# Differential attention's query and key projections ahead of the outputs of gated linear attention, its values and the gate and modulation columns among those outputs

## The chip, the cores and the metric

The kernel runs on one core of one Trainium2 chip. The metric is the time of one execution in device microseconds. The engines are named as in the profile: PE is the matrix engine (PEld its weight loads), DVE the vector engine, ACT the scalar engine, POOL the GpSimd engine, and SP the engine that here only issues transfers.

## What is computed

Two transformer blocks, one after the other, on 512 tokens of width 1024. The part that the change touches is the mixer of the first block. One projection of the normalised tokens (and of 256 context tokens) gives the inputs of two mixers: gated linear attention (GLA, 4 heads), which is evaluated in chunks with a state that decays, and differential attention (4 heads), which is a difference of two softmaxes over 256 + 512 keys.

```python
parts = project(h, w_in)   # gq, gk, gv, gr, gdown, dq, dk, dv
_, _, og = gla_bidir(qg, kg, vg, gf, gb, s_f, s_b)         # forward and backward scan
qd, kd, vd = diff_qkv(parts, q_norm_g, k_norm_g)           # RMS norm of queries and keys
qd, kd = apply_axial_rope(qd, cos, sin), apply_axial_rope(kd, cos, sin)
od = diff_attend(qd, concat(kd_c, kd), concat(vd_c, vd), lam)
mix = concat(gla_merge(og, r), diff_merge(od)) @ w_out     # r is a gate: silu
x = x + gt1 * mix                                          # gt1: a modulation column
```

Modulation columns are the rows of `silu(c) @ w_mod + b_mod`; shifts and scales of the first norm are made at the start, the other 32 columns of 128 in eight jobs of four.

## The kernel before

Matrix products are done in three terms (high and low halves of both sides, rounded to a reduced format): a weight tile is loaded by SP into a ring of two buffers (`wf`), cast by ACT to the high half (`whi`, line 186), and subtracted by DVE to the low half (`wlo`, line 187); those two have rings of three.

The stretch in question has three stages on the time axis.

- The **GLA gates and states** (lines 724 to 814). Gates of the context and of four chunks of 128 tokens, decays, and the states between chunks, in steps that each wait for ACT, DVE and POOL.
- The **GLA outputs** (lines 821 to 920). Sixteen units, one for each chunk and head. A unit takes decays by matrix products (`out_exp`, first line 829), exponentials on ACT (838), products on POOL and DVE (852, 855, 856), a score matrix in 32-column pieces (868 to 878), its assembly (882 to 890), and the output product (898, 899). The products of unit u + 1 are issued before the output of unit u.
- The **differential attention** (lines 924 to 1160 or so). For each head the queries and keys are stacked and transposed (`head_qk`), then 16 steps (4 heads x 4 blocks of 128 queries) of scores, exponentials and outputs; the last instruction of a step's output is the copy of line 1025.

All three leave PE room, and that room is filled from one list, `fillers`, of pairs (cost in us, job). `fill_in(us)` adds its allowance to what is left over and takes jobs off the front while the sum is at least half the cost of the next one. The list in order:

- 32 projection jobs of 24 matrix products of 256 columns each (`tm_job`, lines 284 to 286): keys (`w_dk`, 2 halves x 6 token tiles), values (`w_dv`), queries (`w_dq`, 2 halves x 4 tiles). A key or query job ends in a square on ACT (597), a sum (598), a scaling (602) and, for the tokens that are rotated, one product on DVE (609) and two on POOL (608, 611). A value job ends in one copy on ACT.
- four jobs for the GLA gate `r` (`w_gr`), 24 products of 512 columns each, with three ACT passes and a DVE product (671) at the end.
- modulation jobs (`mod_job`, 331 to 340), eight products in 32 columns of the array and four transposes, with four transfers of 512 KB through the same ring `wf`. `GM` gives the places in the list at which they are inserted; the rest come among the memory inputs (`MM`) and at the end of the list of the attention stage.

`fill_in(8)` stands once behind the context states, `fill_in(FC)` behind each of the four chunk steps, and `FG` is the allowance of an output unit. What is left behind the last unit, less one job, is issued at once; then the attention stage goes on with allowance `FA` a step and its own list (memory keys and values, merges, parts of the output projection).

Of the kernel before, what the change touches and what calls it, by code (L numbers as in the profile page):

```python
# [19 lines left out]
KT = D // 128  # L20
# [7 lines left out]
NLEV = 7  # L28
RW = 1088
GH = 0  # L30
FA, FG, FC, A0, GM, AM, AP = 3.4, 4.6, 3.0, 2, (16, 26), 0, ()
NF = 2
T0 = 1
T1 = 3
NP = 3
FS = 0.6
MM = (0, 1, 3, 5, 7)
NR = 1
GV = 0
PL = 3  # L40
# [21 lines left out]
HO = 0  # L62
# [18 lines left out]
def kernel(ctx: ExitStack, tc: tile.TileContext, a: dict, out: bass.AP, stop=None):  # L81
# [90 lines left out]
    def wsplit(src, n, lo_eng=None, dst=None, shape=None):  # L172
        wf = None if dst is None else dst[2]
        if wf is None:
            wf = ring.tile([128, RW], F32, tag="wf", name="wf", bufs=2)
        if shape is None:
            nc.sync.dma_start(wf[:, :n], src)
        else:
            nc.sync.dma_start(wf[:, :n].rearrange("p (m k c) -> p m k c", m=shape[0], k=shape[1]), src)
        if dst is None:  # L180
            hi = ring.tile([128, RW], F32R, tag="whi", name="whi")
            lo = ring.tile([128, RW], F32R, tag="wlo", name="wlo")
        else:
            hi, lo = dst[:2]
        tc.cur_priority -= WO
        A.copy(hi[:, :n], wf[:, :n])  # L186
        (lo_eng or V).tensor_tensor(lo[:, :n], wf[:, :n], f32(hi[:, :n]), ALU.subtract)  # L187
        tc.cur_priority += WO
        return hi, lo
# [3 lines left out]
    def mm3(o, lhi, llo, rhi, rlo, start, stop):  # L193
        tc.cur_priority += pe_late[0]
        T.matmul(o, lhi, rhi, start=start, stop=False)  # L195
        T.matmul(o, lhi, rlo, start=False, stop=False)  # L196
        ins = T.matmul(o, llo, rhi, start=False, stop=stop).ins  # L197
        tc.cur_priority -= pe_late[0]
        return ins
# [6 lines left out]
    def step():  # L206

        while between:
            try:
                return next(between[0])  # L210
            except StopIteration:
                between.pop(0)

    def drain():
        while between:
            step()

    def fm(w, ms, nk, bhi, blo, alloc, evac, segs=FULL, lo_eng=None, after=None, keep=None, every=4,
           have=None):


        def chunk(m, k0):
            if nk == 4:
                hi, lo = wsplit(w[m // 2].rearrange("p m k c -> p (m k c)"), 1024, lo_eng, keep and keep())
                have[m + 1, 0] = hi[:, 512:], lo[:, 512:]
                return hi, lo
            kn = min(8, nk - k0)
            return wsplit(w[m, :, k0:k0 + kn, :].rearrange("p k m -> p (k m)"), kn * 128, lo_eng, keep and keep())

        have = {} if have is None else have  # L230
        for a_, b_ in segs:
            for m in ms:
                p = alloc(m)
                for k in range(nk):
                    c = (m, k // 8)
                    if c not in have:
                        have[c] = chunk(m, k // 8 * 8)
                    hi, lo = have[c]
                    sl = slice(k % 8 * 128, k % 8 * 128 + 128)
                    mm3(p[:, a_:b_], hi[:, sl], lo[:, sl], bhi(k)[:, a_:b_], blo(k)[:, a_:b_], k == 0, k == nk - 1)  # L240
                    if k % every == every - 1 and k < nk - 1:
                        step()
                evac(m, a_, b_, p[:, a_:b_])
                step()
            if len(segs) > 1:
                drain()
                if after is not None:
                    between.append(after(a_, b_))
# [21 lines left out]
    def tm_load(w, half, n, lo_eng=None):  # L270

        ch = [wsplit(w[half, kc].rearrange("p k n -> p (k n)"), 4 * n, lo_eng) for kc in range(2)]

        def get(k):
            hi, lo = ch[k // 4]
            sl = slice((k % 4) * n, (k % 4 + 1) * n)
            return hi[:, sl], lo[:, sl]
        return get
# [83 lines left out]
    with tc.tile_pool(name="st", bufs=1) as st, tc.tile_pool(name="st2", bufs=2) as st2:  # L362
# [40 lines left out]
        def gq_weights(kc):  # L403

            return wsplit((a["w_gq"][:, :, 4 * kc:4 * kc + 4, :]).rearrange("m p k c -> p m k c"), 1024, shape=(2, 4))

        def gk_weights(kc):
            dst = None
            if kc:
                dst = [wk.tile([128, 1024], F32R, name=f"wk{i}") for i in range(2)] + [None]  # L410
            return wsplit(a["w_gk"][0, kc].rearrange("p k n -> p (k n)"), 1024, dst=dst)
# [51 lines left out]
        w = w0  # L463
        part = projected(0, w0)
        ins = mod_tiles(10)
        for k0 in (2, 4, 6):
            ins = queued(ins, lambda: next(part))
            ins = queued(ins, lambda: mod_tiles(k0))
            if k0 == 4:
                w = gq_weights(1), gk_weights(1)  # L470
# [146 lines left out]
    fillers = []  # L617
    got = {}

    def tm_job(w, hf, t, take, first):  # L620
        def run():
            if first:
                got[w, hf] = tm_load(a[w], hf, 256)
            p = acc()
            if t < 2:
                tm_tile(p[:, :256], got[w, hf], tok(chi, t), tok(clo, t))
            else:
                tm_tile(p[:, :256], got[w, hf], tok(hx, t - 2), tok(hxl, t - 2))
            take(hf, t, p[:, :256], slice(hf * 256, (hf + 1) * 256))
        return run  # L630
# [24 lines left out]
            V.tensor_scalar(rq[:, :, 4 * hf:4 * hf + 4], qk_rms("q", 4).rearrange("p (t h) -> p t h", t=4), 0.125, None, ALU.mult)  # L655

    jobs = [("w_dk", hf, range(6), take_k) for hf in range(2)]
    jobs += [("w_dv", 0, range(2), take_v), ("w_dv", 1, range(6), take_v), ("w_dv", 0, range(2, 6), take_v)]
    jobs += [("w_dq", hf, range(2, 6), take_q) for hf in range(2)]
    for w, hf, ts_, take in jobs:  # L660
        for t in ts_:
            fillers.append((2.6, tm_job(w, hf, t, take, t == ts_[0])))

    got_rs = []

# [4 lines left out]
        sigmoid(e, p)  # L670
        V.tensor_tensor(got_rs[0][:, m], p, e, ALU.mult)
    for m in range(4):
        fillers.append((5.2, lambda m=m: fm(a["w_gr"], [m], KT, hx, hxl, accs, silu_r)))

    def mod_job(n):
        def load(k):
            t = ring.tile([128, RW], F32, tag="wf", name="wm", bufs=2)[:, :1024]
            nc.sync.dma_start(t, a["w_mod"][n, k // 4, :, k % 4:k % 4 + 2].rearrange("p k n -> p (k n)"))
            return t
        return lambda: mod_block(16 + 4 * n, 4, load, mid2)  # L680
    mod_jobs = [(2.6, mod_job(n)) for n in range(8)]
    for at in GM:
        fillers.insert(at, mod_jobs.pop(0))
    left = [0.0]
    late_by = [HO]

    def fill_in(us):

        left[0] += us
        while fillers and left[0] >= 0.5 * fillers[0][0]:  # L690
            cost, run = fillers.pop(0)
            pe_late[0] = late_by[0]
            run()
            pe_late[0] = 0
            left[0] -= cost

    gla_scope = ExitStack()
    gp = gla_scope.enter_context(tc.tile_pool(name="gp", bufs=1))
    gt = gla_scope.enter_context(tc.tile_pool(name="gt", bufs=2))
# [55 lines left out]
    for h in range(4):  # L755
        hs = slice(h * 128, (h + 1) * 128)
        for jt in range(2):
            T.matmul(pU[:, hs], KTs[jt][:, hs], gvc[:, jt, hs], start=jt == 0, stop=jt == 1)
    fill_in(8)

    pg = s2()
    for h in range(4):
# [364 lines left out]
    for k in range(KT):  # L1127
        fillers.append((0.0, lambda k=k: mem_in(k)))
        if k in MM:
            fillers.append(mod_jobs.pop(0))  # L1130
# [699 lines left out]
```

## Time and profile before

| | us |
|---|---|
| median of 3 runs | 1685.4 (1685.23 to 1686.72) |
| the profiled execution | 1684.5 |
| its span, first to last instruction | 1682.7 |
| PE busy in the span | 1608.6 |
| DVE busy | 954.0 |
| ACT busy | 721.7 |
| POOL busy | 385.8 |

Durations below come from the one profiled execution, whose own time is 1684.5 us. PE's busy time counts pipelined products that overlap, so a busy PE can still have room; the distance between the starts of two products is the better measure of what one costs.

### The profile page before, as it was taken

Reading aid. Unit: us, or ns where it says so; the run is one execution under the profiler, and the core shown is the slowest. Engines: PE = TensorE matmul, PEld = TensorE weight load, DVE = VectorE, ACT = ScalarE, POOL = GpSimd, SP = SyncE. Lnnn points to the kernel's source line nnn. Section 1 sums busy time; section 2 is a strip of 40 time slices with the busy share of each in tenths; the row PEclk is TensorE's granted clock in tenths of the full one; section 3 lists DMA queues with packets and bytes.
Section 4 is the critical chain, followed back from the end, with each engine's and each line's share of the span. In section 5 each row is a group of like instructions: output and inputs, shape, how many; then the busy total and the mean of one; then the engine's idle time right before and its main releaser. Section 6 shows DMA issues by size and latency. Waiting matters only on the chain. (4 is left out here: it accounts for less than half of the span.)

```text
span 1682.7 us, 25345 instructions
## 1 busy us (share of the span) xinstructions
PE 1608.6 (96%) x9988; PEld 1355.8 (81%) x9988; DVE 954.0 (57%) x1678; ACT 721.7 (43%) x1372; POOL 385.8 (23%) x402
## 2 busy tenths in 40 slices
PE   8999898989999999999999999999888899999997
PEld 6898787658789888888889777888888888888886
DVE  6548878677656122222335675445677877776233
ACT  4444454567635322232233665234456544444221
POOL 1325546331112221210004000132423222221002
PEclk9999999999999999999999999999899899999998
DMA  9210212353523233323332212335110232333332
GB/s 376 67 48 26 87 55 88 95 188 117 164 78 114 75 101 100 100 91 91 98 111 73 77 37 72 89 99 177 49 36 29 76 99 91 99 99 95 95 91 73
DMA packets 47176, 160.88 MB, mean 96 GB/s; under 512 B 5456, under 2 KB 10064, under 8 KB 45264
## 3 DMA queue, kind: packets, MB, share of 16 engines
q1 hardware_dynamic: 44464, 156.69, 29.8%
q10 hardware_dynamic: 2304, 2.29, 0.4%
q8 instruction: 79, 1.29, 0.3%
q0 software_dynamic: 288, 0.28, 0.1%
q14 instruction: 41, 0.34, 0.1%
HBM read 156.36 MB, written 3.15 MB: 95 GB/s over the span
## 5 line engine op out<-in xcount | busy, mean ns | idle before, releaser
L186 ACT CAST whi<-wf 128x1024 fp32r<-128x1024 f32 (+3 forms) x219 | 226.6, 1036 | 429.2 <-PE acc L196 287.8
L187 DVE TENSOR_TENSOR wlo<-wf,whi 128x1024 fp32r<-128x1024 f32 (+3 forms) x181 | 225.8, 1248 | 180.0 <-ACT whi L186 174.6
L195 PE MATMUL acc<-qhi,whi 128*128 128x512 f32 (+1 forms) x640 | 240.9, 376 | 0.0
L196 PE MATMUL acc<-qlo,whi 128*128 128x512 f32 (+1 forms) x640 | 240.4, 376 | 0.0
L197 PE MATMUL acc<-qhi,wlo 128*128 128x512 f32 (+1 forms) x640 | 240.2, 375 | 0.0
L187 POOL TENSOR_TENSOR wlo<-wf,whi 128x1024 fp32r<-128x1024 f32 x38 | 91.1, 2397 | 209.7 <-ACT whi L186 209.7
L196 PEld LDWEIGHTS acc<-qlo,whi 128*128 128x128 f32 x640 | 122.3, 191 | 19.8 <-issue 0.2
L195 PEld LDWEIGHTS acc<-qhi,whi 128*128 128x128 f32 x640 | 122.3, 191 | 19.7
L197 PEld LDWEIGHTS acc<-qhi,wlo 128*128 128x128 f32 x640 | 122.2, 191 | 19.4
L196 PE MATMUL s<-qlo,whi 128*128 128x512 f32 (+1 forms) x336 | 127.5, 380 | 0.0
L195 PE MATMUL s<-qhi,whi 128*128 128x512 f32 (+1 forms) x336 | 127.5, 379 | 0.0
L197 PE MATMUL s<-qhi,wlo 128*128 128x512 f32 (+1 forms) x336 | 127.3, 379 | 0.0
L1293 DVE TENSOR_TENSOR e<-e,s 128x512 f32<-128x512 f32 (+1 forms) x22 | 14.3, 652 | 153.7 <-PE s L197 153.5
L196 PE MATMUL acc<-glo,whi 128*128 128x512 f32 (+1 forms) x208 | 74.3, 357 | 0.1
L195 PE MATMUL acc<-ghi,whi 128*128 128x512 f32 (+1 forms) x208 | 74.4, 358 | 0.0
L197 PE MATMUL acc<-ghi,wlo 128*128 128x512 f32 (+1 forms) x208 | 74.2, 357 | 0.0
L197 PEld LDWEIGHTS s<-qhi,wlo 128*128 128x128 f32 x336 | 63.2, 188 | 11.8
L195 PEld LDWEIGHTS s<-qhi,whi 128*128 128x128 f32 x336 | 63.2, 188 | 11.8
L196 PEld LDWEIGHTS s<-qlo,whi 128*128 128x128 f32 x336 | 63.2, 188 | 11.8
L195 PE MATMUL acc<-Fhi,whi 128*128 128x512 f32 (+1 forms) x187 | 71.5, 383 | 0.0
L196 PE MATMUL acc<-Flo,whi 128*128 128x512 f32 (+1 forms) x187 | 71.5, 383 | 0.0
L197 PE MATMUL acc<-Fhi,wlo 128*128 128x512 f32 (+1 forms) x187 | 71.5, 382 | 0.0
(643 smaller groups left out, 3994.9 us busy)
## 6 DMA issues: line engine op xcount, KB each, us to landing
wf<-in_w_ffn_in SPq DMA_DIRECT2D x44, 512.0 KB, 3.6
wf<-in_w_up SPq DMA_DIRECT2D x44, 512.0 KB, 3.5
wm<-in_w_mod SPq DMA_DIRECT2D x32, 512.0 KB, 4.1
wm<-in_w_mod SPq DMA_DIRECT2D x8, 1024.0 KB, 13.6
wf<-in_w_ffn_out SPq DMA_DIRECT2D x16, 512.0 KB, 3.5
wf<-in_w_g SPq DMA_DIRECT2D x16, 512.0 KB, 3.6
wf<-in_w_down SPq DMA_DIRECT2D x16, 512.0 KB, 3.5
X<-in_xT SPq DMA_DIRECT2D x4, 1024.0 KB, 5.0
```

What stands on the lines that cost most here:

```text
L186: A.copy(hi[:, :n], wf[:, :n])
L187: (lo_eng or V).tensor_tensor(lo[:, :n], wf[:, :n], f32(hi[:, :n]), ALU.subtract)
L195: T.matmul(o, lhi, rhi, start=start, stop=False)
L196: T.matmul(o, lhi, rlo, start=False, stop=False)
L197: ins = T.matmul(o, llo, rhi, start=False, stop=stop).ins
L1293: V.tensor_tensor(e, e, pu_, ALU.mult)
```

## The change

The list gets a new order and new costs. Keys come first as before, then the values of the context tokens, then the queries, then the values of the other tokens. Ten jobs (`PJ`) are issued as one run ahead of the first GLA gate. The allowance of a chunk step goes from 3.0 to 6.5, that of an output unit from 4.6 to 4.2, that of an attention step from 3.4 to 3.2. Projection jobs are entered at 2.9 instead of 2.6, gate jobs at 5.5 instead of 5.2, modulation jobs at 3.9 instead of 2.6. Four modulation jobs are inserted ahead of the attention stage instead of two, and four stand among the memory inputs instead of five (and one at the end).

```diff
-FA, FG, FC, A0, GM, AM, AP = 3.4, 4.6, 3.0, 2, (16, 26), 0, ()
+FA, FG, FC, A0, GM, AM, AP = 3.2, 4.2, 6.5, 2, (25, 28, 31, 34), 0, ()
+PJ, FP = 10, 8
...
-MM = (0, 1, 3, 5, 7)
+MM = (0, 2, 4, 6)
...
-    jobs += [("w_dv", 0, range(2), take_v), ("w_dv", 1, range(6), take_v), ("w_dv", 0, range(2, 6), take_v)]
+    jobs += [("w_dv", hf, range(2), take_v) for hf in range(2)]
     jobs += [("w_dq", hf, range(2, 6), take_q) for hf in range(2)]
+    jobs += [("w_dv", hf, range(2, 6), take_v) for hf in range(2)]
...
-            fillers.append((2.6, tm_job(w, hf, t, take, t == ts_[0])))
+            fillers.append((2.9, tm_job(w, hf, t, take, t == ts_[0])))
...
-        fillers.append((5.2, lambda m=m: fm(a["w_gr"], [m], KT, hx, hxl, accs, silu_r)))
+        fillers.append((5.5, lambda m=m: fm(a["w_gr"], [m], KT, hx, hxl, accs, silu_r)))
...
-    mod_jobs = [(2.6, mod_job(n)) for n in range(8)]
+    mod_jobs = [(3.9, mod_job(n)) for n in range(8)]
...
+    for _ in range(PJ):
+        fillers.pop(0)[1]()
...
-    fill_in(8)
+    fill_in(FP)
```

On ACT, at the first GLA gate (`gc` is a gate of the context, `qsq` the square that ends a key job, `down` the last input of the gates), before:

```order
L569 COPY down<-mis 32x512
L152 ACTIVATE gc_1071<-mis 128x512
L153 ACTIVATE gc_1071<-gc_1071 128x512
L152 ACTIVATE gc_1082<-mis 128x512
L154 ACTIVATE gc_1071<-gc_1071,ones 128x512
L153 ACTIVATE gc_1082<-gc_1082 128x512
L154 ACTIVATE gc_1082<-gc_1082,ones 128x512
L597 ACTIVATE qsq<-acc 128x256
L750 ACTIVATE ktc<-s_1092 128x512
```

and with the change:

```order
L570 COPY down<-mis 32x512
L598 ACTIVATE qsq<-acc 128x256 x5
L187 CAST whi<-wf 128x1024
L598 ACTIVATE qsq<-acc 128x256
L187 CAST whi<-wf 128x1024
L165 ACTIVATE y_qk<-v_qk 128x24
L166 ACTIVATE y_qk<-y_qk 128x24
L598 ACTIVATE qsq<-acc 128x256 x4
L153 ACTIVATE gc_1435<-mis 128x512
```

Ten key jobs, with the norm of the first half and two weight tiles, now stand between the last input of the gates and the first gate.

On POOL, in the first output units (`QX` and `E` are a unit's own products, `t` and `kdv` those that rotate a key), before:

```order
L852 TENSOR_TENSOR QX<-Rq,q_605 128x384
L608 TENSOR_TENSOR t_1738<-kg,cs_97 128x256
L611 TENSOR_TENSOR kdv<-t_1738,t_1739 128x256
L856 TENSOR_TENSOR E<-E,k_606 128x512
L852 TENSOR_TENSOR QX<-Rq,q_605 128x512
L852 TENSOR_TENSOR QX<-Rq,q_605 128x384
L608 TENSOR_TENSOR t_1839<-kg,cs_97 128x256
L611 TENSOR_TENSOR kdv<-t_1839,t_1840 128x256
L856 TENSOR_TENSOR E<-E,k_606 128x512
```

and with the change, from the fourth unit on:

```order
L861 TENSOR_TENSOR E<-E,k_606 128x512
L857 TENSOR_TENSOR QX<-Rq,q_605 128x512
L857 TENSOR_TENSOR QX<-Rq,q_605 128x384
L727 TENSOR_TENSOR glx_2562<-gx_2560,ghx_2561 128x512
L861 TENSOR_TENSOR E<-E,k_606 128x512
L857 TENSOR_TENSOR QX<-Rq,q_605 128x512
L857 TENSOR_TENSOR QX<-Rq,q_605 128x384
L861 TENSOR_TENSOR E<-E,k_606 128x512
```

From the first product `E` to the end of the units 12 pairs that rotate keys or queries stood on POOL; two are left.

On SP, the transfers from the GLA weights to the memory keys (`wm` modulation, `wf` weights, `lt` constants of the gates), before:

```order
L705 DMA lt_1061<-in_LT 128x896
L708 DMA lt_1064<-in_Lsm 128x512
L177 DMA wf<-in_w_dk 128x1024 x4
L177 DMA wf<-in_w_dv 128x1024 x4
L678 DMA wm<-in_w_mod 128x1024 x4
L177 DMA wf<-in_w_dv 128x1024 x2
L177 DMA wf<-in_w_dq 128x1024 x2
L678 DMA wm<-in_w_mod 128x1024 x4
L177 DMA wf<-in_w_dq 128x1024 x2
L177 DMA wf<-in_w_gr 128x1024 x4
L678 DMA wm<-in_w_mod 128x1024 x20
```

and with the change:

```order
L178 DMA wf<-in_w_dk 128x1024 x4
L710 DMA lt_1425<-in_LT 128x896
L713 DMA lt_1428<-in_Lsm 128x512
L178 DMA wf<-in_w_dv 128x1024 x4
L178 DMA wf<-in_w_dq 128x1024 x4
L178 DMA wf<-in_w_dv 128x1024 x2
L680 DMA wm<-in_w_mod 128x1024 x8
L178 DMA wf<-in_w_dv 128x1024 x2
L680 DMA wm<-in_w_mod 128x1024 x8
L178 DMA wf<-in_w_gr 128x1024 x4
L680 DMA wm<-in_w_mod 128x1024 x16
```

The value weights are now loaded in eight transfers instead of six, and sixteen modulation transfers stand ahead of the gate weights instead of eight.

## Rows read from the trace of the kernel before

**Rows 1.** Head of the page.

```profile
span 1682.7 us, 25345 instructions
```

**Rows 2.** Windows: length, then PE, PEld, DVE, ACT, POOL busy, PE clock, DMA.

```profile
98.00:144.00 46.00, 44.40 (x337) 40.96 (x335) 29.47 (x64) 24.84 (x51) 19.31 (x17) 1.00 0.15 47
144.00:301.00 157.00, 138.33 (x1844) 119.24 (x1844) 130.29 (x225) 71.61 (x192) 88.40 (x76) 0.96 0.22 69
301.00:460.00 159.00, 148.17 (x949) 111.06 (x948) 108.25 (x226) 98.98 (x225) 33.46 (x55) 0.99 0.44 139
```

**Rows 3.** The same view, the stretch of the value jobs.

```profile
212.00:253.00 41.00, 38.35 (x579) 34.48 (x575) 33.18 (x47) 20.32 (x54) 18.83 (x16) 1.00 0.18 57
```

**Rows 4.** Timeline of PE (start, length), starts of output units 0, 7, 11, 12; last output.

```profile
144.02 0.43 PE L829 MATMUL s<-Lr,gx 128*32 128x128 f32 x8
...
211.87 0.43 PE L829 MATMUL s<-Lr,gx 128*32 128x128 f32 x8
...
245.40 0.28 PE L829 MATMUL s<-Lr,gx 128*32 128x128 f32 x1
...
252.61 0.29 PE L829 MATMUL s<-Lr,gx 128*32 128x128 f32 x1
...
300.71 0.38 PE L898 MATMUL mis<-gv,AT 128*128 128x128 f32 x2
```

**Rows 5.** Groups by line in 144 to 301: count, busy us, mean ns, idle before.

```profile
L855 DVE TENSOR_TENSOR QX<-QX,E 128x512 f32<-128x512 f32 x32 | 31.4, 998 | 4.0 <-ACT E L838 3.4
L187 DVE TENSOR_TENSOR wlo<-wf,whi 128x1024 fp32r<-128x1024 f32 x12 | 18.7, 1562 | 1.5 <-ACT whi L186 1.5
L609 DVE TENSOR_TENSOR t<-kg,cs 128x256 f32<-128x256 f32 x12 | 7.7, 638 | 0.4
L598 DVE TENSOR_REDUCE qss<-qsq 128x4 f32<-128x256 f32 x13 | 5.3, 410 | 0.9 <-ACT qsq L597 0.9
L602 DVE TENSOR_TENSOR kg<-acc,rows 128x256 f32<-128x256 f32 x12 | 4.9, 410 | 0.0
...
L608 POOL TENSOR_TENSOR t<-kg,cs 128x256 f32<-128x256 f32 x12 | 13.1, 1091 | 12.8 <-DVE kg L602 8.8 <-DVE v_qk L163 4.0
L611 POOL TENSOR_TENSOR dq__2394<-t,t 128x256 f32<-128x256 f32 x8 | 7.1, 885 | 1.3 <-DVE t_qk L166 0.9
```

**Rows 6.** Timeline of PE, first and last product of one projection job of 24.

```profile
180.64 0.28 PE L284 MATMUL acc<-whi,hc 128*128 128x256 f32 x1
...
183.38 0.28 PE L286 MATMUL acc<-whi,hc 128*128 128x256 f32 x1
```

**Rows 7.** Waits of PE in 144 to 301: total us, times, longest.

```profile
PE acc L285 <- DVE wlo L187: 7.7, 4, 3.2
```

**Rows 8.** Timelines: gate products behind the last unit (48), first stack of queries (DVE).

```profile
301.07 0.48 PE L195 MATMUL acc<-hhi,whi 128*128 128x512 f32 x1
...
311.84 0.39 PE L197 MATMUL acc<-hhi,wlo 128*128 128x512 f32 x1
...
306.39 0.69 DVE L950 CAST sgt<-kdv 128x256 fp32r<-128x256 f32 x1
```

**Rows 9.** Timeline of PE: one of four such groups of a modulation job, its transposes.

```profile
355.98 1.05 PE L331 MATMUL acc<-wm,silc 128*32 128x512 f32 x4
...
359.71 0.60 PE L337 MATMUL acc<-ident,mr 128*128 128x128 f32 x4
```

**Rows 10.** Timeline of ACT: the output copy of attention steps 6 and 16.

```profile
383.23 0.37 ACT L1025 ACTIVATE odn<-mis,rl 128x128 f32<-128x128 f32 x1
...
460.24 0.37 ACT L1025 ACTIVATE odn<-mis,rl 128x128 f32<-128x128 f32 x1 [0.80 <-PE mis L1022]
```

**Rows 11.** Timelines of DVE and POOL around a pair of products in one unit.

```profile
240.88 0.69 DVE L855 TENSOR_TENSOR QX<-QX,E 128x512 f32<-128x512 f32 x1
241.73 1.77 DVE L855 TENSOR_TENSOR QX<-QX,E 128x512 f32<-128x512 f32 x1 [0.15 <-ACT E L838]
...
241.66 1.30 POOL L856 TENSOR_TENSOR E<-E,k 128x512 f32<-128x512 f32 x1 [2.19 <-DVE QX L855]
```

More of the change, by code (lines that the diff above doesn't have):

```diff
@@ L684 @@
     left = [0.0]
-    late_by = [HO]
+    late_by = [0]
     def fill_in(us):
@@ L695, in fill_in @@
             left[0] -= cost
+    for _ in range(PJ):
+        fillers.pop(0)[1]()
+    late_by[0] = HO
     gla_scope = ExitStack()
```

## Prediction, made before the changed kernel was run

> **What bounds the kernel now.** I read the page first, then the windows by stage, then the timeline inside a stage. The span is 1682.7 us [rows 1], and the change moves work only between 98 us (last input of the GLA gates) and 460 us (last attention output), so three windows matter [rows 2]. The reader should see three different limits in them.
>
> In the gates and states, 98 to 144, PE is busy 44.4 of 46.0 us: it is already filled, and whatever is added there lengthens the stage by PE's own price. DVE has 29.5 and POOL 19.3 of the 46.
>
> In the outputs, 144 to 301, DVE is busy 130.3 of 157 us and POOL 88.4, while PE shows 138.3. Sixteen units take 157 us, 9.8 each, but not evenly [rows 4]. The first seven, which carry key jobs, the context's values and one modulation job, take 211.87 - 144.02 = 67.9 us, 9.7 each; the next five, which carry seven or eight value jobs and parts of two modulation jobs, take 252.61 - 211.87 = 40.7, 8.1 each, with DVE at 33.2 of 41 us and POOL at 18.8 [rows 3]; the last four, with query jobs and the first gate job, 300.71 - 252.61 = 48.1, 12.0 each. The units are the same; what differs is what is put between them. A unit with a single value job took 252.61 - 245.40 = 7.2, which I take as the floor of a unit's own chain.
>
> In the attention, 301 to 460, PE shows 148.2 of 159 and no engine is as full as DVE is among the outputs. Steps 6 to 16, which carry memory keys and values, take (460.24 - 383.23) / 10 = 7.7 us each [rows 10].
>
> **The change, part by part.** The order of the program shows that 22 projection jobs stand ahead of the first output instead of 8, that ten of the sixteen units' twelve rotated pieces leave, that all four gate jobs and four modulation jobs come inside the units, and that the attention starts with four modulation jobs and no gate job.
>
> *Gates and states: +40 us.* Fourteen more jobs of 24 products. One job runs from 180.64 to 183.38 plus one more interval of 2.74 / 23 = 0.12, so 2.86 us [rows 6], and 14 x 2.86 = 40.0. No cover exists for it, since PE has only 46.0 - 44.4 = 1.6 us free there. Low end 38 (that idle time is used up). For the high end I suppose that DVE and POOL cannot work beside each other at all in the run of key and query jobs: DVE takes 0.41 + 0.41 + 0.64 for a piece and about 0.5 for its share of weight splits (two of 1.56 for six jobs), POOL 1.09 + 0.89 [rows 5]; together 3.9 against PE's 2.86, so 1.1 more for each of the ten rotated jobs among the fourteen: 51. I take 40, because side by side the two need 2.0 and 2.0, both under 2.86.
>
> *Outputs: -27 us.* Per unit the list now carries ten value or query jobs, four gate jobs and four modulation jobs over sixteen units: 10 x 2.86 = 28.6, 4 x 5.5 = 22.0 (48 gate products take 311.84 - 301.07 plus one interval, so 11.0 for two jobs [rows 8]) and 4 x 4.5 = 18 (four groups a little under 1.05 and transposes of about 0.5 [rows 9]), 68.6 / 16 = 4.3 us. The five middle units carried about 5.5 of the same light kinds at 8.1 a unit. At 8.1 the stage takes 130 instead of 157: -27. A second count goes by DVE [rows 5]: ten pieces of 0.41 + 0.41 + 0.64 leave (-14.6), seven weight splits of 1.56 stand there instead of thirteen (-9.4), three more gate products of about 0.69 come (+2.1, the undisturbed time of that shape [rows 11]); with DVE's idle time as it is, -22. I take -27, since the first count is measured on units with just this kind of filler. Ends: 9.0 a unit, 144 us, -13, if the four modulation jobs hold units as the worst did; 7.2 a unit, 115 us, -42.
>
> *Attention: -22 us.* Three gate jobs (72 products, 16.5 us) and two of six modulation jobs (9 us) leave: 25.5 of PE's time. Not all comes back. The first stack of queries starts at 306.39, behind the last output's norm, 5.3 us after 301.07 [rows 8]; gate products cover that wait now. Afterwards only the first modulation products can, about 2 us, so some 3 us stay: -22. Ends: -28 if modulation jobs also free their places in the ring of weights (four transfers each through two buffers), -11 if half of the removed PE time was only filling waits.
>
> *What costs nothing.* Two more transfers of value weights (512 KB each) fall where the DMA engines are 0.22 busy [rows 2]; their casts and subtractions are in the count of seven above. On SP the last two value tiles now queue behind eight modulation transfers, which wait for PE to free buffers, so a value job can wait for its weights. PE waits four times, 7.7 us in all, for `wlo` now [rows 7]; two such places are left by the new order, so I keep that sum. If it doubles, that is +8, within the high end of the outputs.
>
> *Sum.* +40 - 27 - 22 = -9 us. The profiled execution took 1684.5; 1675.5 follows. The median is 0.9 above it, so 1676.
>
> **Rivals.** *The attention returns nothing* (slower). The 16 steps could be set by their own chain of exponentials, transposes and copies, so that the work that leaves was only filling waits. Then +40 - 27 + 0 = +13, 1698. It decides from the point where the attention gives back less than 13 us. For it speaks that PE's busy time hides gaps in a stage of short products; against it, that steps 6 to 16, which still carry eight projection jobs and a modulation job, (8 x 2.86 + 4.5) / 10 = 2.7 us a step, run at 7.7, well under the 159 / 16 = 9.9 of the whole stage, and that the removed jobs sat in the slow first part.
>
> *DVE and POOL shut each other out in the run of key and query jobs.* +51 - 27 - 22 = +2, 1687. For it: `QX` takes 0.69 alone and 1.77 when a POOL product starts just ahead of it [rows 11]. Against it: in 98 to 144 the two sum to 48.8 us in 46, which leaves room if they overlap at all.
>
> *The outputs fall to their floor.* +40 - 42 - 22 = -24, 1661. For it: the mean of `QX` among the outputs is 998 ns against 0.69 undisturbed [rows 5, 11], and ten pairs of POOL products, 10 x 1.98 = 19.8 us, leave. Against it: each unit keeps its own POOL products, and those meet `QX` in the middle stretch too. The Trainium skill's page "SBUF — State Buffer", section "Who interferes with whom", says that a DVE instruction with two SBUF inputs and a POOL instruction that reads SBUF block each other entirely, whichever starts first. By that rule the 19.8 us that leave POOL come off DVE's waits too, which is this rival; by the same rule the run of key and query jobs is the rival before it. The trace agrees at 241.73: 1.77 is more than the 0.69 by about what POOL's 1.30 leaves to run.
>
> That the change doesn't do what it says is excluded by the order of instructions.
>
> **How the numbers follow.** Forecast 0.54 at 1676 (1668 to 1684); attention returns nothing 0.14 at 1698; engines shut each other out 0.15 at 1687; floor 0.17 at 1661. A measurement of this kernel can tell about 0.2%, 3.4 us, from no change. The band of "same" is 1682.0 to 1688.8. Faster: 0.17 plus 0.50 of the forecast's 0.54, 0.67. Same: 0.04 of the forecast and nearly all of the 0.15, 0.18. Slower: 0.14 and the rest, 0.15. The range runs from the floor rival to between the two slower ones, 1661 to 1692; about a tenth lies above and a tenth below.
>
> **What would show each step.** In the new profile the first output unit should start near 184 instead of 144 (38 to 51 later); the outputs should last about 130 us, the DVE busy time in them near 106 to 108, and a unit near 8.1; the last attention output should come about 137 us behind the last GLA output instead of 159. A first unit later than 195 would mean that DVE or POOL bounds the run of key jobs. Outputs of 145 or more would mean that modulation transfers or late weight splits hold the units, and then PE's waits for `wlo` and `wm` grow. An attention stage of over 147 us would mean that its own chain, not fillers, sets it. From 520 us on nothing should differ.

## The result, and the profile after

The changed kernel takes 1701.4 us (median of four runs, 1695.6 to 1704.4) where the kernel before, beside it, takes 1685.9: a ratio of 1.0088, 95% interval 1.0068 to 1.0108. It is **15.4 us slower**; 9 us faster was forecast, and the time lies above the range. The profiled execution took 1700.2 us. Its span and its windows over the same three stages (length, then busy us of PE, PEld, DVE, ACT, POOL, PE clock, DMA share, GB/s), which answer to [rows 1, 2]:

```profile
span 1698.4 us, 25368 instructions
...
98.00:192.00 94.00, 89.64 (x700) 86.23 (x699) 63.18 (x119) 40.61 (x81) 35.50 (x34) 0.98 0.24 70
192.00:342.00 150.00, 125.43 (x1607) 92.70 (x1606) 103.26 (x183) 65.42 (x178) 69.36 (x59) 0.93 0.27 85
342.00:479.00 137.00, 123.33 (x851) 96.90 (x850) 103.93 (x219) 92.97 (x216) 35.30 (x55) 0.99 0.43 135
```

The boundaries are these rows of the timelines (start, length): the first product of the first output unit, the last output, the last copy of the attention. They answer to [rows 4, 10].

```profile
192.40 0.42 PE L834 MATMUL s<-Lr,gx 128*32 128x128 f32 x8
...
342.00 0.38 PE L903 MATMUL mis<-gv,AT 128*128 128x128 f32 x2
...
478.44 0.37 ACT L1030 ACTIVATE odn<-mis,rl 128x128 f32<-128x128 f32 x1 [1.42 <-PE mis L1027]
```

| us | before | after | change | forecast | PE's price of the jobs moved |
|---|---|---|---|---|---|
| gates and states, from 98 | 46.0 | 94.4 | +48.4 | +40 | +40.0 |
| outputs | 157.0 | 149.9 | -7.1 | -27 | -14.5 |
| attention | 159.2 | 136.1 | -23.1 | -22 | -25.5 |
| behind the attention | 1222.5 | 1220.0 | -2.5 | 0 | 0 |
| span | 1682.7 | 1698.4 | +15.7 | -9 | 0 |

The stages start at 98 us, so the rows of a column and those 98 us make the span. The last column is the reading that was missing. It takes the prediction's own prices (2.86 us for a projection job, 5.5 for a gate job, 4.5 for a modulation job) and counts where jobs left and arrived: fourteen projection jobs out of the outputs, three gate jobs and two modulation jobs from the attention into them. The sum is zero, as it must be when work is only moved on one engine. The forecast's -9 therefore claimed that the three stages would lose 9 us less beyond PE's price. They lost more: 8.4 in the gates, 7.4 in the outputs, 2.4 in the attention. By the heads of the two pages PE is busy 1608.6 us before and 1613.4 after, so 10.9 of the 15.7 us are idle time of PE and 4.8 are longer busy time for the same work.

Among the outputs DVE fell even below the 106 to 108 us foretold: 103.3 us busy instead of 130.3. The stage did not follow. PE's waits there (total us, times, longest), the answer to [rows 7]:

```profile
PE s L873 <- POOL E L861: 10.8, 7, 6.2
PE mis L903 <- DVE AT L895: 5.5, 4, 2.2
PE s L883 <- DVE E L861: 4.5, 4, 1.2
...
PE acc L332 <- DMA wm<-in_w_mod: 1.2, 3, 0.5
PE acc L286 <- DVE wlo L188: 0.8, 1, 0.8
```

The waits for weights, 7.7 us before, are nearly gone, and those for modulation weights are small here (in the attention stage they rose from 3.3 to 7.8 us). What PE waits for now is the units' own chain: POOL's product `E`, the second product `E` on DVE, the assembled scores `AT`. In the kernel before, the wait that answers to the first was this:

```profile
PE s L868 <- POOL E L856: 3.5, 4, 1.7
```

The longest of the new waits, 6.2 us, is in the first unit. The timeline of DVE, POOL, ACT and PE around it:

```profile
192.69 0.41 DVE L599 TENSOR_REDUCE qss<-qsq 128x4 f32<-128x256 f32 x1
...
194.64 0.58 ACT L843 ACTIVATE E<-s 128x512 f32<-128x512 f32 x1
194.75 1.38 DVE L819 SCALAR_TENSOR_TENSOR Sst<-Sst,dec 64x128 f32<-64x128 f32 x3
...
195.73 0.58 ACT L843 ACTIVATE E<-s 128x512 f32<-128x512 f32 x1
196.15 1.22 DVE L188 TENSOR_TENSOR wlo<-wf,whi 128x1024 fp32r<-128x1024 f32 x1
197.29 0.41 DVE L599 TENSOR_REDUCE qss<-qsq 128x4 f32<-128x256 f32 x1
...
198.18 0.97 POOL L609 TENSOR_TENSOR t<-kg,cs 128x256 f32<-128x256 f32 x1 [2.48 <-DVE kg L603]
198.48 1.21 DVE L860 TENSOR_TENSOR QX<-QX,E 128x512 f32<-128x512 f32 x1
199.23 1.05 POOL L612 TENSOR_TENSOR dq__1840<-t,t 128x256 f32<-128x256 f32 x1
...
200.24 1.77 POOL L861 TENSOR_TENSOR E<-E,k 128x512 f32<-128x512 f32 x1
...
202.07 0.80 PE L873 MATMUL s<-QX,E 128*128 128x128 f32 x2 [6.20 <-POOL E L861]
```

The exponentials of the unit were ready at 195.2 and 196.3. But two query jobs stand ahead of its products in the queues of DVE (`qss`, `kg`) and POOL (`t`, `dq`), with the state products of line 819 and a weight split between them. POOL's `E` overwrites what `QX` reads, so it must follow DVE's `QX` of 198.48 as well as the query's `dq`; it starts at 200.24, and PE stands for 6.2 us. The clock falls meanwhile, to the lower of its two levels (0.50, 1.2 GHz). Windows of the time after that, of the first three units and of the other thirteen (the clock is the third figure from the end):

```profile
199.00:207.00 8.00, 4.93 (x74) 3.62 (x74) 3.77 (x5) 0.97 (x3) 5.10 (x5) 0.50 0.15 53
...
192.40:223.40 31.00, 21.82 (x289) 18.56 (x290) 24.98 (x43) 10.43 (x29) 17.21 (x17) 0.78 0.09 29
223.40:342.30 118.90, 103.51 (x1340) 74.36 (x1330) 77.93 (x140) 55.09 (x151) 52.16 (x44) 0.97 0.32 100
```

So the jobs put ahead of the outputs did not only take PE's time in the gates: their tail on DVE and POOL met the first unit. The first three units took 31 us, with 8.6 us of jobs in them as in the kernel before, where they took 24. That holds the stage's loss beyond PE's price: the other thirteen units leave 58.9 us when the price of their jobs is taken off (118.9 less 60.0), and those of before left 58.5 (133.1 less 74.6).

### The profile page after: what moved, and what is told of

The parts are those of the page before. It is cut to its first block, busy times and chain, and to the rows that moved or that the text cites. A ratio compares the mean times of both kernels' runs of the same rounds, so it can differ in the third digit from the quotient of the medians.

```text
span 1698.4 us, 25368 instructions
## 1 busy us (share of the span) xinstructions
PE 1613.4 (95%) x9988; PEld 1358.3 (80%) x9988; DVE 951.1 (56%) x1680; ACT 721.6 (42%) x1374; POOL 384.7 (23%) x402
## 4 chain that ended last, share of the span: by engine, by line
PE 79%; DVE 10%; ACT 4%; DMA 3%; issue 2%; POOL 1%; DVEq 0%; SPq 0%; ACTq 0%; POOLq 0%
PE acc L197 15%; PE acc L196 15%; PE acc L198 15%; PE s L196 5%; PE s L197 5%; PE s L198 5%; PE acc L286 2%; PE acc L285 2%; PE acc L287 2%; PE acc L332 2%; DMA wm<-in_w_mod 1%; DVE wlo L188 1%; PE mis L1027 1%; PE mis L1503 1%; ACT whi L187 1%
## 5 line engine op out<-in xcount | busy, mean ns | idle before, releaser
L187 ACT CAST whi<-wf 128x1024 fp32r<-128x1024 f32 (+4 forms) x221 | 228.5, 1035 | 428.7 <-PE acc L197 292.6
L188 DVE TENSOR_TENSOR wlo<-wf,whi 128x1024 fp32r<-128x1024 f32 (+2 forms) x183 | 227.1, 1241 | 180.1 <-ACT whi L187 174.9
L197 PE MATMUL acc<-glo,whi 128*128 128x512 f32 (+1 forms) x208 | 74.3, 357 | 0.1
```

## The experiments

Each was timed in at least four executions beside the kernel before; the stage lengths are from its profiled execution. The rows in the fences are windows, as above, of the outputs of that run, with the boundaries at its own first unit and last output, unless something else is said.

**Where the jobs ahead stand: runs early and ahead14.** Both keep the 22 jobs ahead of the outputs. Early:

```diff
-PJ, FP = 10, 8
+PJ, FP = 16, 8
...
-        fill_in(FC)
+        fill_in(2.9 if c < 3 else 0)
```

> The changed kernel with the same 22 projection jobs ahead of the outputs, but 16 of them ahead of the gates (10 there in the changed kernel), three after the context's gates and one behind each of the first three state steps, so none behind the last; same products and same outputs. Entry theory: the query jobs in the last state step stand on DVE and POOL ahead of the first output unit; without them the first three units take 24 us instead of 31, no half clock follows, the outputs fall from 150 to 138 or less, the whole to about 1690. Theory that modulation and gate jobs hold the units, and theory that a unit's own chain sets the pace: outputs stay between 147 and 153, the whole within 5 us of 1701.

The first three units took 23.5 us and the outputs 142; PE's first wait for POOL's `E` shrank from 6.2 us to 1.7. The whole took 1695.7 (1.0065, 1.0043 to 1.0086). The size falls between the two theories, since 138 was hoped for, and the half clock did not stay away altogether: it is 0.50 from 201.3 to 204.5. But the entry theory holds: some 7 of the outputs' 150 us were the query jobs in front of the first unit, with the clock that fell behind the stand. The gates and states took 96 us.

```profile
194.00:336.00 142.00, 120.06 (x1592) 87.99 (x1595) 101.14 (x181) 65.24 (x178) 66.58 (x56) 0.98 0.27 87
```

Ahead14 puts all fourteen extra jobs in the run, and leaves between the gates and states as many as before:

```diff
-PJ, FP = 10, 8
+PJ, FP = 14, 8
...
-        fill_in(FC)
+        fill_in((2.9, 2.9, 5.8, 2.9)[c])
```

> The changed kernel with the same 22 projection jobs ahead of the outputs, but the extra fourteen all ahead of the gates; three after the context's gates and one, one, two, one in the four state steps, as in the kernel before. Theory that the changed kernel's extra loss lies where projection jobs crowd the gates, the states and the entry of the outputs (12.7 us of PE time lost in the gates against 6.2 before, 48.5 in the outputs against 40.8): gates and states 88 to 91 instead of 94.4 with 6 to 8 lost, outputs 140 to 144 with 41 to 43 lost, the whole 1686 to 1690, so level with the kernel before. Theory that each job ahead costs more than PE's own price wherever it stands: gates and states stay at 94 to 96, the whole 1693 to 1697 like run early.

The run itself, and then the outputs:

```profile
98.50:138.50 40.00, 39.79 (x330) 39.49 (x329) 24.43 (x50) 11.06 (x24) 14.81 (x16) 1.00 0.31 88
...
189.50:333.50 144.00, 122.56 (x1610) 92.24 (x1608) 100.12 (x181) 65.42 (x178) 67.53 (x57) 0.95 0.27 85
```

In the run PE is busy 39.8 of 40 us at full clock, with 330 products, 2.9 us a job, and DVE and POOL have room. So key jobs do run at PE's price, and the rival in which DVE and POOL shut each other out is gone. The stage still took 91.7 us, 45.7 more than before, where 40 is PE's price: from the first gate product to the first unit it was 50.8 us instead of 46.1, with the same eight jobs in it. PE waits there 1.2 us for DVE's and 1.2 for POOL's part of the context's gates (before, 0 and 0.4), behind the pieces of the run; in all its waits among gates and states grew by 2.7 us. The other half of the 5 us I could not lay at one door. The whole took 1694.1 (1.0059, 1.0037 to 1.0081), not the 1686 to 1690 expected.

**What is put into the units: runs nomod and noboth.** Nomod has no modulation job among the outputs, noboth neither these nor the gate jobs.

```diff
-FA, FG, FC, A0, GM, AM, AP = 3.2, 4.2, 6.5, 2, (25, 28, 31, 34), 0, ()
+FA, FG, FC, A0, GM, AM, AP = 3.2, 3.2, 6.5, 2, (), 0, ()
...
-MM = (0, 2, 4, 6)
+MM = tuple(range(8))
```

Noboth has 1.8 in place of 3.2 there, and `NR = 4` in place of 1.

> The changed kernel with all eight modulation jobs in the attention (none of them among the outputs); ten projection jobs and four gate jobs stay among the outputs. Theory that modulation jobs hold the units: the outputs lose more than the 18 us of PE time that leave, from 150 to 128 or less (under 8 us a unit where no gate job stands), the attention grows by 18 to 22, the whole is 1697 or less. Theory that a unit's own chain sets the pace: the outputs stay at 144 to 150, the attention grows by 18 to 22, the whole is 1713 to 1720. Entry theory: the first three units stay at 31 us, outputs about 135, the whole 1703 to 1710.

> The changed kernel with all eight modulation jobs and the four gate jobs in the attention; only ten light projection jobs among the sixteen output units. It measures a unit with next to nothing put into it. If fillers of the heavy kinds hold the units, outputs about 115 (7.2 a unit, the floor of the prediction), attention 136 + 18 + 22 = 176, the whole about 1706. If a unit's own chain sets the pace, the outputs stay over 140 with PE idle for 80 us of it, attention 176, the whole 1730 or more.

```profile
190.00:323.00 133.00, 108.00 (x1529) 89.79 (x1528) 104.27 (x175) 62.98 (x174) 70.08 (x59) 0.94 0.11 33
```

```profile
190.00:316.00 126.00, 93.76 (x1439) 77.08 (x1431) 100.91 (x169) 56.92 (x164) 72.12 (x59) 0.89 0.10 29
```

Without the modulation jobs the outputs are 17 us shorter, for 18 us of products: PE's price, not more, so these jobs do not hold the units beyond what they cost. Without the gate jobs too, another 20 us of products leave and only 7 us come back: with about ten light jobs the sixteen units take 126 us, 7.9 each, and PE waits 16.0 us for POOL's `E`. That mean has the crowded entry and a clock of 0.89 in it; without the first three units it is 7.7, still above the 7.2 that I had read off one unit. Single units are shorter (5.3 us in the changed kernel, below), so one unit's time says little about a floor. I also missed where the work would go: the attention grew by 3.5 us in nomod, not by 18 to 22, because its allowance `FA` was spent, and the jobs ran behind it (the rest of the span 1240 us instead of 1220). The totals are 1702.8 and 1723.6 us: beyond the price of the jobs moved, noboth lost 14 us among the outputs and 13 behind them.

**The other half of the change alone: run brest.** The kernel before, with the modulation and gate jobs moved and no projection job:

```diff
-FA, FG, FC, A0, GM, AM, AP = 3.4, 4.6, 3.0, 2, (16, 26), 0, ()
+FA, FG, FC, A0, GM, AM, AP = 3.2, 6.0, 3.0, 2, (16, 20, 24, 29), 0, ()
...
-MM = (0, 1, 3, 5, 7)
+MM = (0, 2, 4, 6)
```

> The kernel before with only the other half of the change: two more modulation jobs and three more gate jobs go from the attention into the outputs, no projection job moves ahead of the outputs. If PE's idle time in the outputs of before (157 - 138 = 19 us shown, 41 lost by my count of products) hides them, outputs 160 to 168, attention 137, the whole 1670 to 1677, better than both kernels. If modulation and gate jobs hold the units by their order, outputs 182 or more (25 of PE time in full), attention 137, the whole 1685 to 1690.

```profile
144.50:327.00 182.50, 161.23 (x1954) 134.30 (x1954) 128.66 (x233) 77.90 (x203) 84.92 (x76) 0.96 0.27 85
```

25.5 us of products came in, and the outputs grew by 25.5, to 182.5. The attention fell by 22 to 137.2. The whole took 1687.0 us (1.0009, 0.9997 to 1.002): no change. Nothing of what was put in was hidden, although PE showed 19 us of idle time among the outputs of before. DVE's busy time did not grow (128.7), so it was not more work on DVE that made the stage longer.

**Kind and dealing: runs even, qunits, even2, beven.** In these the jobs of the units are dealt out by hand, on top of run early (`p` a projection job, `m` modulation, `g` gate; a group is a unit):

```diff
-    for at in GM:
-        fillers.insert(at, mod_jobs.pop(0))
+    kind = {"p": fillers[22:32], "m": [mod_jobs.pop(0) for _ in range(4)], "g": fillers[32:]}
+    PLAN = "p p m pp g p m pp g m p g m p p g".split()
+    fillers[22:] = [kind[c].pop(0) for c in "".join(PLAN)]
...
-        fill_in(FG * FS)
+        fill_n(len(PLAN[u]))
...
-        fill_in(FG * (1 - FS))
```

Here `fill_n(n)` takes n jobs off the list. Qunits is the same with the values ahead of the queries in the list; even2 has 18 jobs ahead and 14 projection jobs in the units; beven has 8 and 24.

> The kernel of run early (22 projection jobs ahead of the outputs, none behind the last state step) with the ten projection, four modulation and four gate jobs dealt out one by one over the sixteen output units instead of by kind; the work is the same. In early, units with 3.8 us of products last 5.2, units with 7.5 last 8.1 to 11.7, and units with 9.9 to 10.1 last 13.7 to 14.3: lumps cost more than the empty units give back. Theory that the uneven dealing cost the outputs their gain: outputs 128 to 133 instead of 141.6, the whole about 1685. Theory that each unit loses some 2.6 us of PE time whatever stands in it: outputs 139 to 144, the whole within 4 us of early's 1695.7.

> As run even, but the value jobs stand ahead of the query jobs: six value jobs ahead of the outputs in place of six query jobs, eight query and two value jobs among the units in place of two and eight. Same products and same places of the jobs; only the kind differs: six more rotated pieces (three DVE and two POOL passes each) among the outputs. Theory that rotated pieces hold the units by DVE and POOL: outputs 9 to 18 longer than in run even, gates and states 1 to 4 shorter, the whole 6 to 15 longer. Theory that only PE's work and its dealing out count: all within 3 us of run even.

> As run even, but only 18 projection jobs ahead of the outputs (12 ahead of the gates), so four more query and value jobs, fourteen in all, among the output units, dealt out evenly. Theory that a second light job in a unit costs less there (8.3 us against 6.9 with one, 1.4) than the 2.86 to 3.5 it costs in the gates: gates and states 12 to 14 shorter, outputs 6 longer, the whole 6 to 8 below run even. Theory that the outputs take PE's work plus a fixed loss: both sides cancel, the whole within 3 us of run even. Theory that rotated query pieces hold the units by DVE: outputs 14 or more longer, no gain or a loss.

> The changed kernel's columns (four modulation and four gate jobs among the outputs) and job order, but only eight projection jobs ahead of the outputs as in the kernel before, and the other 24 projection jobs dealt out evenly with those eight over the sixteen units. It asks whether moving projections ahead was of any use. Theory that PE's work and its dealing out set the outputs: 150 to 160, gates and states 46, attention 137, the whole 1657 to 1667. Theory that key and query pieces hold the units by DVE (130 us of it busy in the outputs of before): outputs 175 to 183 as in run brest, the whole 1681 to 1689.

The outputs of even, qunits, even2 and beven, each from its own run:

```profile
194.00:337.00 143.00, 123.79 (x1605) 91.52 (x1605) 101.47 (x184) 65.89 (x180) 64.72 (x56) 0.93 0.28 90
```

```profile
193.50:333.50 140.00, 121.18 (x1594) 90.95 (x1594) 110.88 (x206) 65.53 (x181) 76.69 (x68) 0.94 0.29 92
```

```profile
181.00:326.00 145.00, 125.25 (x1659) 97.05 (x1655) 108.07 (x199) 67.94 (x184) 73.35 (x64) 0.95 0.25 81
```

```profile
144.00:320.00 176.00, 150.16 (x1877) 123.03 (x1876) 128.40 (x232) 77.86 (x201) 87.36 (x76) 0.95 0.27 86
```

Qunits against even bears on DVE. Six more rotated query pieces stand among the outputs in place of six value pieces, DVE is 9.4 us and POOL 12.0 us busier, and the outputs are 3 us *shorter*, not 9 to 18 longer. The whole is 1692.8 us against 1700.3. But two things are in that sum, because the new order also takes the query jobs away from the entry. The first three units took 20.4 us in qunits and 26.9 in even. The other thirteen, with 58.4 us of jobs in both:

```profile
221.21:337.06 115.85, 101.24 (x1345) 77.01 (x1332) 78.86 (x139) 56.21 (x153) 48.95 (x43) 0.96 0.30 96
```

```profile
213.87:333.61 119.74, 103.32 (x1374) 78.60 (x1363) 94.96 (x176) 56.67 (x158) 66.31 (x60) 0.94 0.31 98
```

There the rotated pieces, with 16 us more on DVE, made the units 3.9 us longer, at a clock of 0.94 against 0.96. So they cost something, but far less than DVE's time; and taking them away, which was half the argument of my prediction, returned nothing in the changed kernel, whose thirteen units leave 58.9 us against the 58.5 of before.

Dealing by hand brought nothing either (143.0 against early's 142). Even2 is level with even, 1702.4 us, as the theory of a fixed loss said. Beven's outputs, 176 us, are within the figures that I gave the DVE theory, but by the ledger below they are what its products cost, with 6 us more; a gate job and two projection jobs came behind the last output, and the attention took 155 us instead of 137. The whole took 1697.0. That an even order could not help isn't shown: the order that came out was still in lumps. The PE timeline of two units of the changed kernel shows what a lump looks like (line 883 is the last part of a unit's scores, 286 is in a value job, 834 begins the next unit):

```profile
253.62 0.28 PE L834 MATMUL s<-Lr,gx 128*32 128x128 f32 x1
...
262.65 0.23 PE L883 MATMUL s<-QX,E 128*32 128x32 f32 x2
263.72 0.39 PE L286 MATMUL acc<-wlo,hhi 128*128 128x256 f32 x1 [0.84 <-DVE wlo L188]
...
265.35 0.27 PE L883 MATMUL s<-QX,E 128*32 128x32 f32 x8
...
267.05 0.42 PE L883 MATMUL s<-QX,E 128*32 128x32 f32 x27
...
267.39 0.29 PE L834 MATMUL s<-Lr,gx 128*32 128x128 f32 x1
...
272.65 0.41 PE L834 MATMUL s<-Lr,gx 128*32 128x128 f32 x8
```

Two value jobs cut the scores in three, and the next unit's chain begins some 4 us later for it. This unit, begun at 253.62, takes 13.8 us and the one behind it 5.3: 19.0 for two units with 10.2 us of jobs in them, 4.4 left for each. Four units of before with seven value jobs, 20.0 us, took 245.40 - 211.87 = 33.5 [rows 4], 3.4 left for each. But 4.4 is no more than the mean of the ledger below, 4.6: a lump moves time from one unit to the next, and that it costs time isn't shown.

**The ledger.** For each run the window of the outputs less the price of the jobs that stand in it (counted by their products in the trace, at 2.86, 4.5 and 5.5 us) leaves what the sixteen units themselves take:

| run | outputs us | jobs' price us | left us |
|---|---|---|---|
| before | 157.0 | 83.1 | 73.9 |
| brest | 182.5 | 108.6 | 73.9 |
| early | 142.0 | 66.3 | 75.7 |
| ahead14 | 144.0 | 68.6 | 75.4 |
| even | 143.0 | 66.6 | 76.4 |
| qunits | 140.0 | 67.2 | 72.8 |
| even2 | 145.0 | 70.7 | 74.3 |
| beven | 176.0 | 95.6 | 80.4 |
| after | 150.0 | 68.6 | 81.4 |
| nomod | 133.0 | 50.6 | 82.4 |
| noboth | 126.0 | 30.9 | 95.1 |

Seven runs with very different jobs leave 73 to 76 us, some 4.6 a unit. After and nomod, which share the crowded entry, leave 7 more. Noboth, with the least to fill its units, leaves most. The windows are of one execution each, and the granted clock in them differs (0.89 to 0.98), so a us or two either way says nothing. The forecast of 130 us would have left 61.4.

**What makes the 74 us: runs vexp, bvexp, bswap.** Of PE's waits in the changed kernel and in ahead14 the longest in all is for POOL's half of the key product (line 861; line 856 in the kernel before, where it came second, behind the wait for weights [rows 7]). Bvexp is the kernel before with that half on DVE, and vexp is ahead14 with the same edit:

```diff
-            (V if hf else G).tensor_tensor(E[:, :nl], E[:, :nl], kb...
+            V.tensor_tensor(E[:, :nl], E[:, :nl], kb...
```

In bswap the halves change places: `(G if hf else V)`.

> Run ahead14 with one edit: the first half of each unit's key product, done on POOL so far, is done on DVE like the second. PE's longest named wait among the outputs is for that POOL product (5.3 us in early, 10.8 in the changed kernel). Theory that POOL's part of the unit's chain makes the fixed loss of some 41 us: outputs 6 to 12 shorter than in ahead14, the whole 6 to 12 less and under the kernel before. Theory that the loss is the sum of all steps of the chain and does not hang on that product: outputs within 3 us of ahead14; the waits go over to DVE.

> The kernel before with that same edit, the first half of the key product on DVE instead of POOL; all jobs as before. DVE is 130 of 157 us busy among the outputs there and takes some 16 x 0.7 = 11 us more. Theory that DVE's load sets the outputs of before: outputs 8 to 14 longer, the whole 1693 to 1699. Theory that DVE has room and that the chain sets them: outputs 0 to 8 shorter, the whole 1677 to 1686.

> The kernel before with the two halves of each unit's key product exchanged: the first half on DVE instead of POOL, the second on POOL instead of DVE, so neither engine's share of work changes much (bvexp put both on DVE and took the outputs from 157 to 151.3 and the whole 0.31% under the kernel before). Theory that it is the length of the chain up to the first scores that counts, PE's wait for POOL's first half being its largest step: outputs 149 to 153, the whole 1677 to 1682 as in bvexp. Theory that bvexp gained by relieving POOL (88 to 66 us busy): outputs 155 to 160, the whole 1683 to 1688. Theory that the second half on POOL becomes the late one: PE's waits for the second scores grow over bvexp's 6.5 us, no gain.

The outputs of vexp, of bvexp and of bswap; the last two with PE's waits in a fence of their own (line 878 takes the second half's scores, 868 the first's, 285 is in a projection job):

```profile
189.00:326.00 137.00, 120.53 (x1606) 90.17 (x1606) 96.34 (x197) 64.39 (x177) 45.85 (x41) 0.96 0.28 90
```

```profile
144.50:296.00 151.50, 135.75 (x1847) 117.22 (x1845) 124.82 (x241) 71.13 (x192) 66.29 (x60) 0.98 0.23 71
```

```profile
PE s L878 <- DVE E L856: 6.5, 7, 1.9
PE acc L285 <- DVE wlo L187: 2.6, 3, 1.1
```

```profile
146.00:299.00 153.00, 139.46 (x1845) 121.62 (x1844) 112.92 (x225) 71.65 (x192) 80.35 (x76) 0.94 0.23 70
```

```profile
PE s L878 <- POOL E L856: 6.4, 7, 1.7
PE acc L285 <- DVE wlo L187: 2.2, 1, 2.2
...
PE s L868 <- DVE E L856: 1.2, 3, 0.7
```

By the ledger, 68.4 us are left in vexp, 68.4 in bvexp and 69.9 in bswap, instead of 74 to 75. The same edit is worth nearly the same with the old order and with the new, 5.5 and 7.0 us (in bvexp the clock is 0.98 against 0.96 before, so some of its 5.5 can be that). Bswap leaves POOL nearly its whole share (80 us busy of 88 before) and gains almost as much, so what counts is not POOL's load but where in a unit its product stands.

By which way it counts, PE's waits tell differently. In vexp the wait for the first half fell from ahead14's 8.3 us to 3.5, which is most of the gain. In the kernel before the waits for the two halves were 3.5 and 3.2; in bvexp they are 0.8 and 6.5, in bswap 1.2 and 6.4, in sum no less. What fell there is the wait for weight splits, from 7.7 [rows 7] to 2.6 and 2.2. So the product on POOL held the first scores, or held DVE and with it the split that a projection job waits for; which of the two weighs more these runs don't tell. The whole: vexp 1688.3 us, 5.8 under ahead14 but not under the kernel before; **bvexp 1679.8** (ratio 0.9969, 0.9954 to 0.9984) and **bswap 1680.0** (0.997, 0.9959 to 0.9982). Both beat the kernel before and the changed one, with the old order of jobs.

## Why the prediction was wrong

**The step that failed is the outputs, -27, measured -7.1.** It fell in two parts. Some 12.5 us of the -27 were not work that left, but the belief that the units would lose less. I took 8.1 us a unit from the five middle units of before and gave the value jobs the credit for it. The five carried 25 us of jobs, 5.0 a unit and not 5.5 (eight value jobs and half a modulation job), so 3.1 us were left for each; all sixteen left 4.6, and early and ahead14, with the new order and a clearer entry, left 4.7. The ledger shows a loss that hardly depends on the kind of the jobs (qunits) or on their number from 66 to 109 us (brest); one stretch of five units was too small a sample, next to neighbours that took 9.7 and 12.0. The second count, by DVE's busy time, erred in the same way: DVE fell to 103 us, more than counted, and its idle time grew instead. Single terms of it were off too: twelve weight splits [rows 5] were taken as thirteen and became eight, not seven, and 8.9 us of the second `E`, below, were not in it. The other 7 us are the entry: the prediction looked for a limit of DVE and POOL *inside* the run of jobs and not at what the last jobs leave in their queues for the first unit. Early and ahead14 take that away, and 142 to 144 us remain, near the 142.5 that PE's price alone gives.

**Gates and states, +40, measured +48.4.** The price of a job was right, 2.9 us in the run. What was missing is what the run does to the gates behind it: ahead14, which has the same eight jobs among the gates as before, still takes 45.7 more than before, and about half of the 5.7 us beyond the price is named by PE's waits for DVE and POOL; the other half stays open. The remaining 3 us of the changed kernel came with the twelve jobs that it puts among gates and states instead of eight.

**Attention, -22, measured -23.1.** Right: its fillers cost nearly their price. Brest gives the same -22 without the rest. The 3 us that were to stay at the first stack are there as a wait of PE of 4.1 us behind the last output, but it is for modulation weights (347.70 in the changed kernel). The rival in which the attention returns nothing is out.

**The other rivals.** A unit start later than 195 would have shown DVE and POOL as the bound of the run; it came at 192.4, and the run is PE's. The floor of 7.2 a unit was misread: that unit held, beside its value job, half a modulation job, and PE waited for nothing in it, so its time was PE's work and not the chain's:

```profile
250.13 1.59 PE L331 MATMUL acc<-wm,silc 128*32 128x512 f32 x8
```

As a mean it was also too low: noboth, nearly empty, took 7.9. Of the forecast's own tests, the one for outputs over 145 us misled: it laid them to weights, and PE's waits for weights fell.

**The rule on DVE and POOL.** The groups by line among the outputs (busy us, mean ns), of the changed kernel, of the kernel before, of bvexp and of qunits:

```profile
L860 DVE TENSOR_TENSOR QX<-QX,E 128x512 f32<-128x512 f32 x32 | 33.4, 1048 | 7.7 <-ACT E L843 6.8
...
L861 DVE TENSOR_TENSOR E<-E,k 128x384 f32<-128x384 f32 x16 | 13.5, 847 | 0.4
```

```profile
L856 DVE TENSOR_TENSOR E<-E,k 128x384 f32<-128x384 f32 x16 | 22.4, 1398 | 0.4
```

```profile
L855 DVE TENSOR_TENSOR QX<-QX,E 128x512 f32<-128x512 f32 x32 | 27.6, 861 | 1.1 <-ACT E L838 0.9
```

```profile
L867 DVE TENSOR_TENSOR QX<-QX,E 128x512 f32<-128x512 f32 x32 | 26.2, 833 | 3.8 <-ACT E L850 3.3
```

`QX` took 998 ns on average among the outputs of before [rows 5] and 1048 here, with ten rotated pairs less on POOL; without POOL's first half of the key product it took 861 in bvexp, 795 in bswap, and 784 in vexp against 1016 in ahead14. So the rotated pairs were not what held `QX`, and the unit's own POOL product does hold it. But in qunits, with that product in its place, the mean is 833 as well: how much is held hangs on what happens to meet, and the means alone don't divide it. The Trainium skill's page "SBUF — State Buffer", section "Who interferes with whom", says that a DVE instruction with two SBUF inputs contends with a POOL instruction that reads SBUF. The means above the 0.69 of an undisturbed `QX` [rows 11], and their fall where that POOL product leaves, agree with it. But what such contention costs the stage was another matter: with the rotated pairs gone, the second `E` on DVE fell from 1398 to 847 ns, and from the fourth unit on the units were no faster (58.9 us left against 58.5).

**The clock.** The four spans of the changed kernel follow its granted clock: 1693.7 us at a mean of 0.987, 1698.4 at 0.983, 1700.7 at 0.980, 1702.5 at 0.979. Runs of the kernel before lie mostly between 0.985 and 0.989. So some of the 15.4 us goes with the clock, for which the prediction had no term. How much of it is caused by the new order's idle time, and how much varies from run to run, the runs don't separate.

## What to carry to other kernels

When an engine is busy almost all the time, moving its work between stages gives back in one about what it costs in the other (here 40 us for each fourteen jobs); write the ledger of that engine first, and let a forecast of gain name the idle time that will end. A stage with a chain in every unit can have a loss per unit that the choice of fillers leaves nearly alone: look for a product that stands in the unit's way (here one, 4 us of the whole) before re-dealing what fills it. And look at the tail of moved work on the other engines' in-order queues, where the next stage begins.

## What was not expected of the hardware

With a single stand of PE of 6.2 us, from 195.9, came the lower clock: 0.50 in the window from 199 to 207, in which the first scores of the new stage ran. In early, with a wait of 1.7 us at the same place, the clock was at that level for 3 us instead of 10, and over the outputs it is 0.98 against 0.93. The other surprise is how little a busy share says about room: PE showed 18.7 us idle among the outputs of before [rows 2], and 25.5 us of products put there in brest took 25.5 us.
